# Order of the seven products in pairs of weight chunks, place of the softmax exponentials, and buffers kept between stages, in a two-layer diffusion trunk

## The chip, the core and the metric

The kernel runs on one core of one Trainium2 chip. The metric is the device time of one execution in microseconds (us), the median of several runs. Besides these there is one execution that was recorded by the hardware profiler.

## What is computed

A trunk of two layers serves 128 context tokens and 512 latent tokens, 640 columns in all, with a model width of 2048. Both layers have the same frame:

```python
h = rms_norm(x, norm_g[l]) * (1.0 + scale) + shift
y, side = even_mixer(...)  # layer 0; odd_mixer in layer 1
x = x + gate * (y @ w_out[l])
...
y = jnp.concatenate([ya, yb], axis=-1) * jax.nn.silu(gp)   # in both mixers, of h @ w_in
```

`scale`, `shift` and `gate` come from a small product of a conditioning vector (the modulation). The even mixer holds windowed attention with a sink (8 heads) and gated linear attention (4 heads). The odd mixer holds neighbourhood attention on a grid (8 heads) and a spatial gating MLP (gMLP). Each mixer's width is 2048, and its gate `gp` multiplies it. All is float32. Results are the two outputs and the keys, values and states of the context.

## The kernel before

**Chunks.** Activations lie transposed in SBUF: 16 tiles k of 128 features, 640 columns each. A weight chunk is 128 output features wide and 16 tiles k deep. Each float32 operand is split into a high and a low part, both read by TensorE in one pass: activations in `acth` and `actl` (`ah`, `al` in the code), weights in `whi` and `wlo`. A product of one tile is three matmuls of about 320 columns: `acth,whi`, `actl,whi`, `acth,wlo`. Of the weights, ScalarE (ACT) makes `whi`, then GpSimd (POOL) or VectorE (DVE) subtracts to get `wlo`; the split parts lie in a ring of 2560 columns (five pieces of 512, `RING`), so that splits run a few pieces ahead of TensorE (`wpump`, line 727). All loads are queued on SyncE, in order; a load waits there until its buffer is free, and those behind it wait too.

**Pairs.** Most chunks of the second half of the run are taken two at a time (`spair`, line 933), by a scheme of Strassen and Winograd: the tiles k are cut into a near half (0 to 7) and a far half (8 to 15), the columns into halves 1 and 2, and instead of eight half products there are seven. The two chunks c1 and c2 give four corners of weights: 11 and 12 are c1 with the near and the far half of k, 21 and 22 are c2. Sums of corners, made on VectorE by `strassen_jobs` (line 646) in five buffers of 128x1024 (`rs`, `wraw`), are S1 = 21 + 22, S2 = S1 - 11, S4 = 12 - S2, S3 = 22 - S2. The products are A11, A12, S4 and S3 with activations, and S1, S2 and A22 with three sums of activations (numbers 0, 1 and 2). `steps` (line 632) writes their order by hand. A name with a prime is the half of a product with k tiles 4 to 7 of its eight, without a prime tiles 0 to 3. Each such half is one block of 12 matmuls; a pair of full form has 14 blocks. Some pairs are of a short form (`ns` = 4), in which only 4 tiles of each half take part and the others are plain products.

The three sums of activations for tiles 0 to 3 stay in SBUF (`eh`, `el`). Those for tiles 4 to 7 lie in DRAM (`far_dram`) and come through four slots (`tail`), one set at a time: the primed halves of S1, S2 and A22 read the slots, and behind each tile the slot is loaded again with the set that the next of them needs (`far_load`, line 928). The order of a full pair is

`A11' A11 S1' S1 A12 A12' S4 S2' S2 S4' S3 S3' A22' A22`,

so each pair loads all three sets, 12 loads. There are 28 full pairs: a run of 24 in the odd layer's input projection (5 with the gMLP, 13 with the neighbourhood attention, 6 with gates) and 4 in the last output projection. `fold` (line 1101) makes the sums ahead of a run and puts one of them in the place of half 2 of the near tiles of `acth` and `actl`, for S3 (`t_dram` in the trace); the originals are kept in DRAM (`bh_dram`, `bl_dram`) and come back in `unfold` (line 1255), which is called behind the last pair of a run (lines 2425 and 2597).

Results gather in PSUM banks. Five are for the pairs (`npj`). A bank t holds A11, then S2 and S3 on top of it; between them ScalarE copies it out (`copy`, line 1008, to `sums`), after all pending evacuations were forced (`settle`). Evacuations are generators in a queue (`later`); they add the copies to the banks and pass the result to the chunk's own function (`lin`, `gate`, `out_evac`).

**Order of the work.** The whole program is laid out by a planner (`Pace`, and `tick`, line 479): TensorE's pair blocks are written in order, and behind every second tile pieces of other work (attention heads, splits, folds, the modulation) are emitted, when the planner's own estimate of engine and DMA times says that their inputs are ready. A DMA is reckoned in `dma` (line 416). `until` yields until an estimate has come; `wait` until a flag stands; `need` runs other tasks without emitting pair blocks until a flag stands.

**Heads.** Both attentions go through `blocks` (line 1674): for each block of 128 queries `s1` makes the scores and `soft1` (line 1651) the maximum `mx`, its negative `nm` on VectorE and the exponential on ScalarE; `soft2` scales; two blocks later `s3` transposes. At the end of a head, transposed blocks meet the values in matmuls of up to 512 columns (`bank<-Y 128x512` in the trace). In the neighbourhood attention, `open_na` (line 2536) first needs the gMLP to be done, closes its buffers and opens others; `open_g1` (line 2572) needs the last head, closes these, opens the gate's buffers and loads parked tiles of y.

Of the kernel before, what the change touches and what calls it, by code (L numbers as in the profile page):

```python
# [22 lines left out]
T = NCTX + NLAT  # L23
# [210 lines left out]
class Trunk:  # L234
# [177 lines left out]
    force = busy = False  # L412
# [3 lines left out]
    def dma(self, out, in_):  # L416
# [7 lines left out]
        def emit():  # L424
            at = pc.t["q"] = max(pc.t["q"], self.now, pc.ready("q", o, i)) + 0.45
            pc.t["d"] = max(pc.t["d"], at + 0.65) + max(0.09, n / 360e3)
            pc.note("q", o, i, pc.t["d"] + 1.0)
            self.nc.sync.dma_start(out, in_)  # L428
# [203 lines left out]
    def steps(c1, c2, ns):  # L632

        if ns == NS:
            todo = "A11' A11 S1' S1 A12 A12' S4 S2' S2 S4' S3 S3' A22' A22".split()
# [10 lines left out]
    def strassen_jobs(self, pairs):  # L646
# [11 lines left out]
        free[4] = len(J)  # L658
        if len(pairs) > 1:
            J.append(load(4, pairs[1][0], 0))  # L660
        for n, (c1, c2, ns, *_) in enumerate(pairs):
            one, two = (pairs[n + i] if n + i < len(pairs) else None for i in (1, 2))
            spare = ({*range(5)} - {*at.values()}).pop()
            sums = {
# [3 lines left out]
                "S3": ("21", "22", "11", ALU.subtract),  # L668
            }
            home = {"A11": "11", "A12": "12", "S1": "21", "S2": "11", "S4": "12", "S3": "21", "A22": "22"}  # L670
            when = {
                ("A11", 1): [("S1", 1), ("S2", 1)],
                ("A11", 0): [("S1", 0), ("S2", 0)],
                ("A12", 0): [("S4", 0)],
                ("A12", 1): [("S4", 1)],
                ("S4", 0): [("S3", 0)],
                ("S2", 1): [("S3", 1)],
            }
            if ns != NS:
                when = {("A12", 0): [("S1", 0), ("S2", 0)], ("S1", 0): [("S4", 0), ("S3", 0)]}  # L680
            steps = self.steps(c1, c2, ns)
            todo = list(steps)
            next_at = {"11": spare}
            for key in steps:
# [6 lines left out]
                J.append(("split", key, lambda i=at[home[f]], h=h: self.piece(i, h), 4, 128))  # L691
                for g, i in when.get((f, h), ()):
                    o, a, b, op = sums[g]
                    J.append(("add", lambda x=(at[o], at[a], at[b]), i=i: [self.piece(y, i) for y in x], op))
                if f not in [x[1] for x in todo] and f in ("S2", "S4", "S3", "A22"):
                    i = at[home[f]]
                    free[i] = len(J)
                    r = {"S2": "21", "S4": "22", "S3": "12", "A22": None}[f]
                    if r and one:
                        next_at[r] = i  # L700
                        J.append(load(i, one[int(r[0]) - 1], NS * (int(r[1]) - 1)))
                    elif r is None and two:
                        J.append(load(i, two[0], 0))
# [229 lines left out]
    def spair(self, c1, c2, ns, used, then):  # L933
# [17 lines left out]
        def tt(f):  # L951
# [31 lines left out]
        def product(b, view, key, x, again=None):  # L983
            hi, lo = self.wget(key)
            st = first(b)
            for i in range(4):
# [3 lines left out]
                if i % 2:  # L990
                    self.tick()
# [39 lines left out]
        def two(x, v):  # L1031
            yield from self.until(x)
            plus(x, half(v))
# [16 lines left out]
        t = take()  # L1050
        xa = xb = v = ya = None
        steps = self.steps(c1, c2, ns)
        for n, key in enumerate(steps):
            c, f, h = key
            last = f not in [x[1] for x in steps[n + 1 :]]
            if isinstance(f, int):
# [3 lines left out]
                else:  # L1060
                    ya = ya or take()
                    plain(key, ya, v)
                if c == c1 and f > NS:
                    later(c1, one(xa, x))
            elif f == "A11":
                product(t, full, key, J(x1))
                if last:
                    x = copy(full(t))
            elif f == "A12":
                xa = xa or take()  # L1070
                product(xa, full, key, M(x1))
                if last and ns == NS:
                    later(c1, one(xa, x))
            elif f == "S1":
# [4 lines left out]
            elif f == "S2":  # L1079
                product(t, full, key, tt(1), 2)  # L1080
                if last:
                    x = copy(half(t))
                    later(c1, two(x, v))
            elif f == "S4":
                xb = xb or take()
                product(xb, half, key, M(x2))
                if last:
                    later(c1, three_(xb, x))
            elif f == "S3":
                self.need(f"T3{h}")  # L1090
                product(t, half, key, J(x2))
                if last:
                    x = copy(full(t))
                    self.drop(t)
            else:
                ya = ya or take()
                product(ya, full, key, tt(2), 0 if then else None)
                if last:
                    later(c2, four(ya, v, x))
# [551 lines left out]
    def soft1(self, p, ps, mask, w, sinkcol):  # L1651
# [22 lines left out]
    def blocks(self, n, s1, s3, lag, hold):  # L1674
# [5 lines left out]
        for t in range(n + lag):  # L1680
# [11 lines left out]
            if t < n:  # L1692
# [4 lines left out]
                st[t] = s1(t, own[t])  # L1697
# [1198 lines left out]
```

## Time and profile before

| | |
|---|---|
| runs of the kernel before | 2179.47, 2179.72 and 2186.09 us, median 2179.72 |
| profiled execution | 2187.29 us |
| its span on the core | 2185.5 us |
| instructions | 39032 |
| HBM read and written | 403.10 MB, 38.45 MB |
| mean granted TensorE clock | 0.987 |

A profile row of a group or the timeline reads: line, engine, operation, written tile <- read tiles, shapes, count, and in brackets the idle time of that engine just before and what ended it. Line 208 is that of a helper through which all instructions of VectorE, ScalarE and GpSimd pass, 394 that of matmuls, 399 that of transposes, 428 that of loads; so tiles tell more than lines. In rows of windows stand the bounds, the width, busy time and count of TensorE's matmuls, its weight loads, VectorE, ScalarE and GpSimd, then the granted clock of TensorE (1.00 is full), the share of busy DMA time and GB/s.

### The profile page before, as it was taken

Reading aid. Unit: us, or ns where it says so; the run is one execution under the profiler, and the core shown is the slowest. Engines: PE = TensorE matmul, PEld = TensorE weight load, DVE = VectorE, ACT = ScalarE, POOL = GpSimd, SP = SyncE. Lnnn points to the kernel's source line nnn. Section 1 sums busy time; section 2 is a strip of 40 time slices with the busy share of each in tenths; the row PEclk is TensorE's granted clock in tenths of the full one; section 3 lists DMA queues with packets and bytes.
Section 4 is the critical chain, followed back from the end, with each engine's and each line's share of the span. In section 5 each row is a group of like instructions: output and inputs, shape, how many; then the busy total and the mean of one; then the engine's idle time right before and its main releaser. Section 6 shows DMA issues by size and latency. Waiting matters only on the chain.

```text
span 2185.5 us, 39032 instructions
## 1 busy us (share of the span) xinstructions
PE 2083.0 (95%) x13990; PEld 1992.6 (91%) x13990; DVE 1537.5 (70%) x3389; ACT 959.0 (44%) x2084; POOL 1021.9 (47%) x775
## 2 busy tenths in 40 slices
PE   7999999999999999999899999999999999998896
PEld 5789999999899999999899998999899899998896
DVE  1337777767887876788647877887777777665565
ACT  4425445343433445444444344444444544443343
POOL 3433233323223222566365655554545466647793
PEclk9999999999999999999999999999999999999998
DMA  9934433346445334776576677777776686665786
GB/s 375 360 135 151 130 109 99 103 129 201 135 127 175 120 117 138 242 235 204 154 241 213 226 266 245 263 242 245 242 247 215 224 286 237 217 211 193 235 273 214
DMA packets 232819, 446.76 MB, mean 204 GB/s; under 512 B 27376, under 2 KB 93744, under 8 KB 232624
## 3 DMA queue, kind: packets, MB, share of 16 engines
q1 hardware_dynamic: 231152, 442.70, 60.7%
q8 instruction: 110, 1.80, 0.3%
q10 hardware_dynamic: 1472, 1.56, 0.2%
q14 instruction: 85, 0.70, 0.1%
HBM read 403.10 MB, written 38.45 MB: 202 GB/s over the span
## 4 chain that ended last, share of the span: by engine, by line
PE 67%; DMA 11%; DVE 10%; issue 5%; POOL 3%; ACT 3%; SPq 1%; ACTq 0%; POOLq 0%; DVEq 0%
PE bank L394 64%; DMA tail<-far_dram 2%; POOL wlo L208 2%; DVE arena L208 2%; DVE Y L208 2%; PE bank L399 2%; DVE adas L208 1%; PE bank L1510 1%; DMA rs<-w_odd 1%; DVE bank L208 1%; SPq L428 1%; DMA wraw<-w_odd 1%; DMA adas<-ada_g 1%; DVE wlo L208 1%; DVE actl L208 1%
## 5 line engine op out<-in xcount | busy, mean ns | idle before, releaser
L394 PE MATMUL bank<-acth,whi 128*128 128x320 f32 (+1 forms) x3144 | 968.4, 319 | 24.5 <-DMA acth<-bh_dram 6.5
L394 PE MATMUL bank<-acth,wlo 128*128 128x320 f32 (+1 forms) x3144 | 942.4, 311 | 4.9 <-POOL wlo L208 3.2
L394 PE MATMUL bank<-actl,whi 128*128 128x320 f32 (+1 forms) x3144 | 941.0, 311 | 1.5 <-DMA actl<-bl_dram 1.5
L208 POOL TENSOR_TENSOR wlo<-wraw,whi 128x512 fp32r<-128x512 f32 x370 | 518.2, 1409 | 781.2 <-ACT whi L208 668.9
L394 PEld LDWEIGHTS bank<-acth,whi 128*128 128x128 f32 x3144 | 586.1, 189 | 44.1 <-ACT whi L208 7.3
L394 PEld LDWEIGHTS bank<-acth,wlo 128*128 128x128 f32 x3144 | 585.0, 189 | 7.9 <-POOL wlo L208 5.1
L394 PEld LDWEIGHTS bank<-actl,whi 128*128 128x128 f32 x3144 | 586.2, 189 | 3.4 <-DMA actl<-bl_dram 1.9
L208 POOL TENSOR_TENSOR wlo<-rs,whi 128x512 fp32r<-128x512 f32 x244 | 343.0, 1417 | 257.6 <-ACT whi L208 209.7
L208 ACT ACTIVATE whi<-wraw 128x512 fp32r<-128x512 f32 (+1 forms) x429 | 261.7, 623 | 166.6 <-PE bank L394 94.7
L208 ACT ACTIVATE whi<-rs 128x512 fp32r<-128x512 f32 x297 | 179.2, 623 | 76.3 <-PE bank L394 41.1
L208 DVE CUSTOM_DVE_ANT_0 adas<-adas,bank,partg 128x256 bf16<-128x256 f32 (+1 forms) x320 | 178.1, 557 | 19.9 <-ACT bank L208 7.1
L394 PE MATMUL bank<-tail,whi 128*128 128x322 f32 (+1 forms) x672 | 159.2, 323 | 16.4 <-DMA tail<-far_dram 11.1
L394 PE MATMUL bank<-eh,wlo 128*128 128x322 f32 (+1 forms) x444 | 139.4, 314 | 1.8 <-DVE wlo L208 1.2
L394 PE MATMUL bank<-eh,whi 128*128 128x322 f32 (+1 forms) x444 | 141.0, 318 | 0.0
L394 PE MATMUL bank<-el,whi 128*128 128x322 f32 (+1 forms) x444 | 138.8, 313 | 0.0
L394 PEld LDWEIGHTS bank<-tail,whi 128*128 128x128 f32 x672 | 112.8, 192 | 25.0 <-DMA tail<-far_dram 16.5
L208 ACT ACTIVATE Y<-bank 128x128 f32<-128x128 f32 (+5 forms) x134 | 52.4, 411 | 135.7 <-PE bank L394 82.8
L208 ACT ACTIVATE bc<-bank 128x2 f32<-128x2 f32 (+1 forms) x101 | 17.1, 170 | 210.8 <-DVE arena L208 124.3
L394 PE MATMUL bank<-tail,wlo 128*128 128x322 f32 (+1 forms) x336 | 105.7, 315 | 3.5 <-POOL wlo L208 3.5
L208 DVE TENSOR_TENSOR rs<-rs 128x512 f32<-128x512 f32 x81 | 90.3, 1125 | 25.6 <-POOL wlo L208 19.5
L208 DVE TENSOR_TENSOR wlo<-wraw,whi 128x512 fp32r<-128x512 f32 x59 | 62.8, 1066 | 62.7 <-ACT whi L208 57.5
L208 DVE TENSOR_TENSOR bank<-bank,sums 128x320 f32<-128x320 f32 (+1 forms) x148 | 69.6, 493 | 40.0 <-PE bank L394 39.6
(215 smaller groups left out, 2952.1 us busy)
## 6 DMA issues: line engine op xcount, KB each, us to landing
tail<-far_dram SPq DMA_DIRECT2D x288, 322.0 KB, 4.8
wraw<-w_even SPq DMA_DIRECT2D x176, 256.0 KB, 3.2
adas<-ada_g SPq DMA_DIRECT2D x128, 256.0 KB, 4.4
adas<-ada SPq DMA_DIRECT2D x128, 256.0 KB, 3.7
rs<-w_odd SPq DMA_DIRECT2D x60, 512.0 KB, 6.5
wraw<-w_odd SPq DMA_DIRECT2D x40, 512.0 KB, 6.0
Y<-ada SPq DMA_DIRECT2D x37, 512.0 KB, 6.7
rs<-w_out SPq DMA_DIRECT2D x30, 512.0 KB, 4.7
```

The costliest lines, as they stand in the source:

```text
L208: return f(*args, **kw)
L394: self.nc.tensor.matmul(out, lhsT, rhs, start=start, stop=stop, **kw)
L399: self.nc.tensor.transpose(out, in_, self.ident[:k, :k])
L428: self.nc.sync.dma_start(out, in_)
L1510: nc.tensor.matmul(o, c, w[:, j, :], start=(q == 0), stop=(q == 3))
```

## The change

**Alternating pairs.** The full pairs of a run now have three orders: an opening pair (`back` None), then pairs that run backward and forward in turn (`back` True and False):

```diff
-            todo = "A11' A11 S1' S1 A12 A12' S4 S2' S2 S4' S3 S3' A22' A22".split()
+            if back is None:
+                todo = "A11' A11 A12 A12' S1' S1 S4' S4 S2 S2' S3 S3' A22 A22'".split()
+            else:
+                todo = "A11' A11 A12 A12' S2' S2 S4' S4 S3 S3'".split()
+                todo = ["A22'", *todo, "A22", "S1", "S1'"] if back else ["S1'", "S1", *todo, "A22", "A22'"]
```

A forward pair ends with set 2 of the far sums in the slots, and the backward pair that follows begins with it; a backward pair ends with set 0, with which the forward one begins. Each of them loads two sets, 8 loads.

```diff
-                product(t, full, key, tt(1), 2)
+                product(t, full, key, tt(1), 0 if back else 2)
...
-                product(ya, full, key, tt(2), 0 if then else None)
+                product(ya, full, key, tt(2), 1 if back else None)
```

In a backward pair S1 comes last and is added to bank t, so that t is copied four times, not three, and the results of c1 and c2 are put together by other generators (`five`, `six`, `seven`):

```diff
+            elif f == "S1" and back:
+                product(t, half, key, tt(0, 2))
+                if last:
+                    x = copy(half(t))
+                    later(c1, six(xb, x))
+                    later(c2, seven(t))
```

The loads of corners go in the order in which the next pair needs them, and S1 of a forward pair is added on VectorE while the pair before it is still under way, behind the split of A22:

```diff
+        order = lambda p: ("11", "21", "22", "12") if p[4] is None else ("22", "11", "21", "12") if p[4] else ("21", "22", "11", "12")
...
+                if back and (f, h) == ("A22", 1):
+                    add("S1", 1)
+                    add("S1", 0)
...
+                if one and one[4] is False and key == steps[-3]:
+                    add("S1", 1, next_at)
+                    add("S1", 0, next_at)
```

On SyncE, in the gate stage of the odd layer, the loads of the far sums (`tail`) and of corners (`rs`, `wraw`) stood before as:

```order
L428 DMA tail_10968<-far_dram 128x644 x12
L428 DMA wraw<-w_odd 128x1024
L428 DMA rs_7767<-w_odd 128x1024 x2
L428 DMA wraw<-w_odd 128x1024
L428 DMA tail_10968<-far_dram 128x644 x8
L428 DMA rs_7767<-w_odd 128x1024
L428 DMA tail_10968<-far_dram 128x644 x2
```

Now, in the same stage:

```order
L428 DMA tail_11102<-far_dram 128x644 x8
L428 DMA rs_7781<-w_odd 128x1024 x3
L428 DMA wraw<-w_odd 128x1024
L428 DMA tail_11102<-far_dram 128x644 x8
L428 DMA rs_7781<-w_odd 128x1024 x2
L428 DMA wraw<-w_odd 128x1024
L428 DMA tail_11102<-far_dram 128x644 x8
```

Between as many corner loads there are fewer far loads; over the program 336 became 232.

**Unfolding.** It is started behind S3 of a run's last pair and no longer behind that pair:

```diff
+                    if end:
+                        self.spawn(self.unfold(), first=True)
...
-            do(lambda: (self.turn_tail(False), self.spawn(self.unfold(), first=True)))
+            do(lambda: self.turn_tail(False))
```

At the end of layer 0's output projection, SyncE's rows were (the returned originals are `bh_dram` and `bl_dram`, `x1T_dram` is the spill of x):

```order
L428 DMA wraw<-w_out 128x512
L428 DMA tail_81<-x1T_dram 128x640
L428 DMA x1T_dram<-arena_7774 128x640
L428 DMA tail_81<-x1T_dram 128x640
L428 DMA arena_7774<-xT 128x640
L428 DMA acth<-bh_dram 128x320
L428 DMA actl<-bl_dram 128x320
```

and are now, from the last of the returned tiles on:

```order
L428 DMA acth<-bh_dram 128x320
L428 DMA actl<-bl_dram 128x320
L428 DMA adas<-crow_s 128x2x256
L428 DMA wraw<-w_out 128x512
L428 DMA tail_81<-x1T_dram 128x640
L428 DMA x1T_dram<-arena_7788 128x640
L428 DMA tail_81<-x1T_dram 128x640
L428 DMA arena_7788<-xT 128x640 x2
```

The returned tiles moved ahead of the last spill and of the two loads around it.

**Exponentials.** `soft1` is a generator now and yields until the planner's time for nm has come, before it emits the exponential:

```diff
+        yield from self.until(nm)
         self.act(p[:, :w], p[:, :w], AF.Exp, bias=nm, accum_out=den)
```

**Planner.** A DMA's reckoned time grows:

```diff
-            pc.t["d"] = max(pc.t["d"], at + 0.65) + max(0.09, n / 360e3)
+            pc.t["d"] = max(pc.t["d"], at + 1.2) + max(0.09, n / 330e3)
```

**Buffers in place.** The neighbourhood heads use the gate's buffers (`ssq`, `last`, `xr`) and no others are opened; the flags "gmlp" and "nh7" are waited for by the tasks and evacuations that touch the buffers, and the parked tiles of y are loaded by a task:

```diff
         def open_na():
-            self.need("gmlp")
-            self.close_arena()
-            self.arena(4.61)
-            L["hq"], L["hk"] = self.take(T, 2), self.take(T, 2)
+            L["hq"], L["hk"] = Ring([self.ssq, self.last[:, :T]]), Ring(self.xr.list)
...
         def open_g1():
-            self.need("nh7")
-            self.close_arena()
-            for i in range(4):
-                self.dma(Y[:, 8 + i, :], ysp[:, i, :])
-            for i in range(6):
-                self.dma(Y[:, 2 + i, :], self.hsp[:, i, :])
-            self.open_gate()
+            def homes():
+                yield from self.wait("nh7")
+                for i in range(4):
+                    self.dma(Y[:, 8 + i, :], ysp[:, i, :])
+                    self.flags.add(f"home{8 + i}")
+                    yield
...
+            self.spawn(homes(), first=True)
```

Where the last head ends, TensorE's rows were (`eh` is a block of S2 or A22 or S1; `ident` are transposes of the head's last block, then come its products with the values):

```order
L394 MATMUL bank_70<-eh_7765,wlo 128x322
L399 MATMUL bank_73<-ident,arena_12619 128x128
L399 MATMUL bank_73<-ident,arena_12619 64x128
L399 MATMUL bank_73<-ident,arena_12619 128x128
L394 MATMUL bank_72<-Y 128x512
L394 MATMUL bank_72<-Y 128x128
L394 MATMUL bank_72<-Y 128x256 x3
L394 MATMUL bank_72<-Y 128x128
L394 MATMUL bank_69<-acth,whi 128x322
```

and are now:

```order
L394 MATMUL bank_68<-eh_7779,wlo 128x322
L399 MATMUL bank_72<-ident,Y 128x128 x3
L399 MATMUL bank_73<-ident,arena_7788 128x128
L399 MATMUL bank_73<-ident,arena_7788 64x128
L399 MATMUL bank_73<-ident,arena_7788 128x128
L394 MATMUL bank_72<-Y 128x512
L394 MATMUL bank_72<-Y 128x128
L394 MATMUL bank_72<-Y 128x256 x3
L394 MATMUL bank_72<-Y 128x128
L394 MATMUL bank_69<-acth,whi 128x320
```

They moved from the border between the last pair with attention and the first with gates to the middle of the latter, and the transposes of the block before the last have come next to them.

More of the change, by code (lines that the diff above doesn't have):

```diff
@@ L411 @@
     share, soon = 0.0, 99.0
-    force = busy = False
+    force = busy = often = False
     lags2, cap2 = (8.0, 6.0, 4.0, 1.0, 0.4), 2.0
@@ L658, in strassen_jobs @@
         free[4] = len(J)
+        order = lambda p: ("11", "21", "22", "12") if p[4] is None else ("22", "11", "21", "12") if p[4] else ("21", "22", "11", "12")
+        corner = lambda i, p, r: load(i, p[int(r[0]) - 1], NS * (int(r[1]) - 1))
         if len(pairs) > 1:
-            J.append(load(4, pairs[1][0], 0))
-        for n, (c1, c2, ns, *_) in enumerate(pairs):
+            J.append(corner(4, pairs[1], order(pairs[1])[0]))
+        for n, pair in enumerate(pairs):
+            c1, c2, ns, _, back = pair
             one, two = (pairs[n + i] if n + i < len(pairs) else None for i in (1, 2))
             spare = ({*range(5)} - {*at.values()}).pop()
+            last = "11" if back else "21"
             sums = {
@@ L680, in strassen_jobs, with add @@
                 when = {("A12", 0): [("S1", 0), ("S2", 0)], ("S1", 0): [("S4", 0), ("S3", 0)]}
-            steps = self.steps(c1, c2, ns)
+            elif back is None:
+                when["A11", 1].insert(0, ("S1", 1))
+                when["A11", 0].insert(0, ("S1", 0))
+            steps = self.steps(c1, c2, ns, back)
             todo = list(steps)
-            next_at = {"11": spare}
+            rest = list(order(one)) if one else []
+            next_at = {rest.pop(0): spare} if one else {}
+            def add(g, i, at=at):
+                o, a, b, op = sums[g]
+                J.append(("add", lambda x=(at[o], at[a], at[b]): [self.piece(y, i) for y in x], op))
             for key in steps:
@@ L1029, in one, with two @@
             self.drop(xa)
-        def two(x, v):
-            yield from self.until(x)
-            plus(x, half(v))
+        def two(x, y):
+            yield from self.until(x, y)
+            plus(x, y)
         def three_(xb, x):
@@ L1048, in four, with five, six, seven @@
             self.drop(ya, v)
-        t = take()
-        xa = xb = v = ya = None
-        steps = self.steps(c1, c2, ns)
+        def five(ya, xb, x):
+            yield from self.until(x)
+            plus(full(ya), x)
+            nc.vector.tensor_tensor(half(xb), half(xb), half(x), ALU.subtract)
+            yield from ev(c2, ya, None)
+            self.drop(ya)
+        def six(xb, x):
+            yield from self.until(x)
+            plus(half(xb), x)
+            yield from ev(c1, None, half(xb))
+            self.drop(xb)
+        def seven(t):
+            yield from ev(c2, None, half(t))
+            self.drop(t)
+        t = xa = xb = v = ya = None
+        steps = self.steps(c1, c2, ns, back)
         for n, key in enumerate(steps):
@@ L1079, in spair @@
             elif f == "S2":
-                product(t, full, key, tt(1), 2)
+                product(t, full, key, tt(1), 0 if back else 2)
                 if last:
                     x = copy(half(t))
-                    later(c1, two(x, v))
+                    if not back:
+                        later(c1, two(x, half(v)))
+                    if back is None and ns == NS:
+                        later(c1, three_(xb, x))
             elif f == "S4":
@@ L1086, in spair @@
                 product(xb, half, key, M(x2))
-                if last:
-                    later(c1, three_(xb, x))
+                if last and (back is not None or ns != NS):
+                    later(c1, two(half(xb), x) if back else three_(xb, x))
             elif f == "S3":
@@ L2550, in open_na @@
             L["nk"] = Ring([yt(1, 256) for _ in range(2)])
-            self.pieces = [yt(1, 384) for _ in range(3)] + [self.take(384)]
+            self.pieces = [yt(1, 384) for _ in range(3)] + [self.last[:, T:]]
         do(open_na)
```

83 lines of the change are left out of this document (46 added, 37 removed).

## The prediction

> **What bounds the kernel now.** I read the page first, then the list of who waited for whom on TensorE, then the timeline around the longest waits, then windows for the price of a wait. From the page:
>
> ```profile
> span 2185.5 us, 39032 instructions
> PE 2083.0 (95%) x13990; PEld 1992.6 (91%) x13990; DVE 1537.5 (70%) x3389; ACT 959.0 (44%) x2084; POOL 1021.9 (47%) x775
> ```
>
> TensorE (PE) works 2083 of 2185.5 us. The order of both kernels holds the same number of matmuls, so only the 102 idle us and the time at a reduced clock can change. The list of waits names who ended the idle time (us in total, times, longest):
>
> ```profile
> PE bank L394 <- DMA tail<-far_dram: 11.1, 9, 4.2
> PE bank L394 <- ACT whi L208: 9.9, 7, 3.2
> PE bank L394 <- POOL wlo L208: 7.2, 9, 1.4
> PE bank L394 <- DMA acth<-bh_dram: 6.5, 2, 4.3
> ```
>
> No one wait rules: the top row is the reload of the far operands, rows two and three are weights split too late, the last the unfolding. The timeline puts the longest waits in their places (start, duration, idle before in brackets):
>
> ```profile
> 1058.69 0.63 PE L394 MATMUL bank<-acth,whi 128*128 128x320 f32 x1 [4.31 <-DMA acth<-bh_dram]
> 1061.09 0.64 PE L394 MATMUL bank<-actl,whi 128*128 128x320 f32 x1 [1.50 <-DMA actl<-bl_dram]
> 1911.80 0.58 PE L394 MATMUL bank<-acth,whi 128*128 128x320 f32 x1 [2.19 <-DMA acth<-bh_dram]
> 2035.54 0.56 PE L394 MATMUL bank<-tail,whi 128*128 128x320 f32 x2 [1.05 <-DMA tail<-far_dram]
> 2040.49 0.90 PE L394 MATMUL bank<-tail,whi 128*128 128x320 f32 x2 [4.24 <-DMA tail<-far_dram]
> ```
>
> A wait costs more than its idle time. In the windows the first number behind the bounds is the width, the second TensorE's busy time with its matmuls, the last but two the granted clock:
>
> ```profile
> 1030.00:1050.00 20.00, 20.00 (x138) 20.00 (x137) 13.03 (x50) 8.49 (x16) 13.57 (x11) 1.00 0.47 148
> 1059.00:1066.00 7.00, 5.50 (x22) 5.10 (x22) 0.82 (x1) 0.74 (x1) 0.00 (x0) 0.54 0.78 176
> 1242.00:1248.00 6.00, 6.00 (x37) 6.00 (x36) 3.35 (x4) 1.48 (x3) 3.49 (x3) 0.72 0.07 11
> 1354.00:1360.00 6.00, 5.02 (x22) 4.75 (x23) 1.81 (x5) 0.63 (x1) 1.27 (x1) 0.72 1.03 377
> 1553.00:1559.00 6.00, 5.21 (x28) 4.89 (x28) 3.18 (x8) 1.83 (x5) 3.91 (x3) 0.72 0.52 150
> 1912.00:1918.00 6.00, 6.00 (x31) 5.99 (x32) 1.02 (x2) 1.70 (x3) 0.00 (x0) 0.72 0.92 298
> 1976.00:1982.00 6.00, 5.59 (x28) 5.33 (x27) 5.86 (x5) 3.15 (x6) 5.92 (x6) 0.72 0.32 112
> 2040.00:2046.00 6.00, 5.51 (x24) 5.51 (x24) 0.00 (x0) 1.26 (x2) 1.94 (x2) 0.58 0.74 258
> ```
>
> The first window is undisturbed: 20 us / 138 = 0.145 us a matmul, so a block of 12 is 1.74 us. In the others, busy time x (1 - clock) is lost on top of the wait: 5.50 x 0.46 = 2.5 us, then 1.7, 1.4, 1.5, 1.7, 1.6 and 2.3 us.
>
> The Trainium skill, TensorE: Matmul & The Clock Gate, section "What's actually happening", says that the clock falls to half after at least one idle window of about 3.4 us. This trace differs: 0.72 stands after an idle of only 2.19 us. By that rule only the waits of 4.31 and 4.24 us would cost clock, the clock's part of the sum below (8.9 us) would be 3.5, and the result 2161 us.
>
> **The change part by part.** The sum is made against the profiled execution (2187.3 us, span 2185.5); the median of the runs, 2179.7, lies 7.6 lower, and I take what is saved off that.
>
> *Unfolding earlier.* SyncE's timeline shows why it was late:
>
> ```profile
> 1050.98 0.33 SPq L428 DMA_DIRECT2D x1T_dram<-arena  x1
> 1054.39 0.32 SPq L428 DMA_DIRECT2D tail<-x1T_dram  x1
> 1055.28 0.39 SPq L428 DMA_DIRECT2D acth<-bh_dram  x1
> ```
>
> The load stood behind a load that waited for a spill, and was issued 0.9 us after TensorE had run dry (1058.69 - 4.31 = 1054.38). Now it is queued after S3 of the last pair and ahead of those two. What is left of that pair is a plain block of 24 matmuls and A22, 36 x 0.145 = 5.2 us; at the second place, whose pair runs backward, A22, S1 and S1', 5.2 us too. The waits were 4.31 + 1.50 and 2.19, with 2.5 + 1.7 of clock: 12.2 us. I take 11, since 5.2 doesn't quite cover 5.8. Bounds 6 (VectorE is late next at the first place) and 12.
>
> *Alternating pairs.* TensorE keeps its 168 matmuls a pair. The far loads fall from 336 to 232. The rows for landing (KB each, us):
>
> ```profile
> tail<-far_dram SPq DMA_DIRECT2D x288, 322.0 KB, 4.8
> rs<-w_odd SPq DMA_DIRECT2D x60, 512.0 KB, 6.5
> ```
>
> Before, A22' reloaded its slots three blocks ahead of S1', 5.2 us against 4.8 for landing: no margin. Now the shortest distance is four blocks (A22' to S2' backward), 7.0 us, the others five to seven; three remain only once, in each opening pair. So I take away all tail waits but those of the run that opens the last projection: 11.1 - (1.05 + 4.24) = 5.8, and 1.4 of clock. In that opening pair S1' now comes 24 matmuls later, behind A12: 3.5 of its 5.3 us go, and 1 of 2.3 of clock. Together 11.7; bounds 7 (the opening pair gains nothing) and 15 (its wait goes whole).
>
> Its costs. In the opening pair S3 follows S2' on the same bank with nothing between, so TensorE waits for ScalarE's copy: 0.42 us of copy (the sums row below) and the way there and back, 0.7 x 2 pairs = 1.4 us. Backward pairs copy once more, 14 x 0.42 = 5.9 us on ScalarE, hidden in its 56% idle time; uncovered it would be the whole 5.9. A forward pair's S1 is now added in the pair before, after the split of A22, and its corner 22 is loaded only after the split of S4, three splits earlier: 3 x 1.74 = 5.2 us against 6.5 for landing. Before, five splits lay between. The nearest rows are VectorE's waits for such corners:
>
> ```profile
> DVE rs L208 <- DMA rs<-w_odd: 5.0, 3, 2.9
> DVE wraw L208 <- DMA wraw<-w_odd: 4.5, 3, 1.8
> DVE rs L208 <- DMA wraw<-w_odd: 3.9, 2, 3.5
> DVE wraw L208 <- DMA rs<-w_odd: 2.7, 2, 2.5
> ```
>
> That is 16.1 / 10 = 1.6 us each; at 12 borders 19 us of VectorE. Queued behind the waiting add are evacuations, for which ScalarE and the next splits wait. Five weight slots ahead of TensorE (2560 / 512, some four blocks, 7 us) cover most; I let a quarter through, 5 us, with bounds 0 and 52 (the first rival).
>
> *Exponentials when their maximum is ready.* ScalarE waited for that maximum (nm) often, and once TensorE can be seen behind it:
>
> ```profile
> ACT arena L208 <- DVE nm L208: 89.4, 47, 4.5
> ACT Y L208 <- DVE nm L208: 53.7, 30, 4.3
> 1550.59 0.56 ACT L208 ACTIVATE arena<-arena,nm 128x320 f32<-128x320 f32 x1 [1.35 <-DVE nm L208]
> 1552.72 0.57 PE L394 MATMUL bank<-tail,whi 128*128 128x322 f32 x2 [2.13 <-ACT whi L208]
> ```
>
> The split of the weights (whi) stood behind the exponential on ScalarE: 2.13 us and 1.5 of clock, 3.6. Of 143 us of such waiting the rest is hidden; I add 1.4 for both attention stages and take 5. Bounds 2 and 12. The added wait is the generator's, not an engine's: a head gets longer by the ticks until nm is there. What then is late is the end of a head.
>
> *Longer DMA times in the planner.* ScalarE's conversions were queued before the store that still read their tile had landed:
>
> ```profile
> 1971.78 0.47 ACT L208 ACTIVATE Y<-adas 128x320 fp32r<-128x320 f32 x1 [3.57 <-DMA far_dram<-Y]
> 1975.70 0.41 PE L394 MATMUL bank<-acth,whi 128*128 128x320 f32 x1 [3.17 <-ACT whi L208]
> 2017.54 0.47 ACT L208 ACTIVATE Y<-Y 128x320 fp32r<-128x320 f32 x1 [6.11 <-DMA t_dram<-Y]
> 2018.28 0.42 ACT L208 ACTIVATE sums<-bank 128x320 f32<-128x320 f32 x1
> 2019.27 0.41 PE L394 MATMUL bank<-acth,whi 128*128 128x320 f32 x1 [2.63 <-DVE sums L208]
> ```
>
> 3.17 + 1.6 + 2.63 = 7.4 us hang on this. The planner's allowance grows by 0.55 us and a little per byte, less than these ScalarE waits: I take half, 4; bounds 0 and 7.4.
>
> *Buffers in place.* The first removed pause leaves no long wait of its own in the timeline. At the second stands
>
> ```profile
> 1744.42 1.90 PE L394 MATMUL bank<-Y 128*128 128x512 f32 x2 [3.74 <-ACT Y L208]
> ```
>
> but the order after shows the last head's final transposes and products still without pair products between, now forced by a gate that is evacuated; I count nothing. The same happens newly at the end of head 2: between nothing and 3.74 us, I take 1.5.
>
> Sum: 11 + 11.7 + 5 + 4 - 1.4 - 5 - 1.5 = 23.8 us. 2187.3 - 23.8 = 2163.5 for the profiled execution, 2179.7 - 23.8 = 2156 for the median.
>
> **The rivals.**
> *Corner 22 comes too late (slower).* If landing with the wait for GpSimd ahead of it takes longer than 5.2 us plus the cover of 7, VectorE stands, evacuations and splits behind it, and TensorE waits at every forward border. The price is that of the worst weight wait in the trace:
>
> ```profile
> 1239.78 0.42 PE L394 MATMUL bank<-acth,whi 128*128 128x322 f32 x1 [1.16 <-ACT whi L208]
> 1241.79 0.42 PE L394 MATMUL bank<-acth,wlo 128*128 128x322 f32 x1 [1.44 <-POOL wlo L208]
> ```
>
> 1.16 + 1.44 + 1.7 of clock = 4.3 us, x 12 = 52, against savings of 31.7 - 2.9 = 28.8: 2179.7 + 23.2 = 2203. It decides from 2.4 us a border. Against it: 6.5 us for landing lies far below 12.
>
> *Gains given back at the transitions.* With the data there, the first place waits for VectorE (7 of its 8.3 us come back), and the exponentials and planner's times bring nothing, as new orders bring their own collisions: 23.8 - 7 - 9 = 7.8 saved, 2172.
>
> *The weight waits go as well.* Four sums in a row after A11 become two, spread over the pair. Then of 9.9 + 7.2 those not counted yet (less 2.13 and 3.17) go, 11.8, with 1.7 of clock, and the 5 at the borders: 18.5 more, 2137.
>
> **How the numbers follow.** Mine 0.44, gains given back 0.22, weight waits too 0.24, corner late 0.10. A measurement of this kernel can tell some 0.3% (6.5 us) from no change; given back lies at 7.8, so over a third of it falls within: faster 0.81, same 0.10, slower 0.09. The range runs from 2134, a little under the weight rival, to 2176, a little above the given-back one.
>
> **What would show it.** Right: the two waits for bh_dram gone or under 1 us; the tail row at 2 to 3 us and only in the last projection; the nm rows of ScalarE near nothing; clock losses at fewer places. Wrong: VectorE's rows for corner loads far above 35 us with whi waits at each forward border; or new whi, sums or transposition waits of a us or two spread over the attention stage, which eat what the loads gave.

## The result and the profile after

The changed kernel takes 2151.57 us (median of four runs, 2148.37 to 2152.63), the kernel before 2181.45 us beside it: a ratio of 0.9858, with a 95% interval of 0.9837 to 0.9878. That is 30 us saved where 23.8 were forecast, inside the range. The profiled execution took 2151.12 us against 2187.29 before, 36.2 less; some 6 us of that are scatter, since the profiled execution before lay 5.8 us above the median of its kernel and the one after 0.5 us below.

The first lines of the page after:

```profile
span 2149.3 us, 38899 instructions
PE 2069.3 (96%) x13990; PEld 1985.7 (92%) x13990; DVE 1533.2 (71%) x3383; ACT 964.8 (45%) x2100; POOL 1033.0 (48%) x781
```

The matmuls are the same in number. TensorE's idle time fell from 102.5 to 80.0 us, its busy time by 13.7 us. The list of waits on TensorE after (us in total, times, longest):

```profile
PE bank L394 <- POOL wlo L208: 10.1, 17, 1.2
PE bank L394 <- ACT whi L208: 8.1, 7, 3.9
...
PE bank L394 <- DMA tail<-far_dram: 6.5, 2, 5.1
...
PE bank L394 <- DVE tail L208: 3.9, 1, 3.9
```

The rows for `bh_dram` and `bl_dram` are gone; the far operands' row fell from nine waits to two. New are more and shorter waits for `wlo`, and one for VectorE's `tail`. The timeline has the long ones in their places:

```profile
1082.16 0.78 PE L394 MATMUL bank<-acth,whi 128*128 128x322 f32 x2 [3.92 <-DVE tail L208]
1941.14 0.63 PE L394 MATMUL bank<-acth,whi 128*128 128x320 f32 x1 [3.93 <-ACT whi L208]
2005.32 0.90 PE L394 MATMUL bank<-tail,whi 128*128 128x320 f32 x2 [5.14 <-DMA tail<-far_dram]
```

To see where the time went, I cut both executions at three marks that stand in every trace with the same matmuls between them: the matmul behind a wait of 1.3 us for `arena` early in each output projection (1 and 3), and the matmul behind the first wait for `whi` of the odd layer's input projection (2). In each row behind the bounds stand the width, then TensorE's busy time with its matmuls, as in the prediction. Between the marks, before:

```profile
859.10:1106.90 247.80, 238.98 (x1582) 235.23 (x1582) 188.13 (x443) 114.00 (x245) 126.27 (x105) 0.99 0.64 203
1106.90:1938.00 831.10, 797.50 (x5203) 767.81 (x5203) 624.21 (x1387) 376.93 (x844) 452.41 (x326) 0.99 0.71 240
1938.00:2185.50 247.50, 217.27 (x1423) 213.20 (x1423) 144.32 (x204) 97.90 (x192) 170.51 (x138) 0.95 0.70 233
```

After:

```profile
857.40:1103.00 245.60, 237.64 (x1581) 234.56 (x1581) 187.48 (x432) 112.79 (x243) 124.53 (x101) 0.99 0.64 199
1103.00:1902.70 799.70, 781.55 (x5203) 759.71 (x5203) 626.93 (x1369) 381.95 (x858) 475.70 (x340) 1.00 0.64 212
1902.70:2149.30 246.60, 217.25 (x1423) 213.27 (x1423) 146.22 (x209) 97.59 (x194) 161.11 (x133) 0.96 0.66 217
```

The second row of each is the finding: of 36 us, 31.4 come from the stretch 2 to 3, which holds the 24 pairs of the odd layer with the neighbourhood attention beside them. There idle time fell by 15.4 us (831.10 - 797.50 = 33.6, then 18.2). In windows of 1 us, busy time x (1 - clock) adds up to 11.2 us of lost clock there before and 1.7 after. Of the waits in that stretch, those for ScalarE's `Y` fell from 7.3 to 1.9 us, for `whi` from 6.7 to 2.5, for the far operands from 5.4 to 1.4, and the 2.2 us for `bh_dram` went; those for VectorE's `arena` rose from 0.6 to 3.6. The stretch with the first unfolding gave 2.2 us, the last projection 0.9.

### The profile page after: what moved, and what is told of

Its sections match the earlier page's. It is cut to its first block, busy times and chain, and to the rows that moved or that the text cites. A ratio compares the mean times of both kernels' runs of the same rounds, so it can differ in the third digit from the quotient of the medians.

```text
span 2149.3 us, 38899 instructions
## 1 busy us (share of the span) xinstructions
PE 2069.3 (96%) x13990; PEld 1985.7 (92%) x13990; DVE 1533.2 (71%) x3383; ACT 964.8 (45%) x2100; POOL 1033.0 (48%) x781
## 5 line engine op out<-in xcount | busy, mean ns | idle before, releaser
L208 POOL TENSOR_TENSOR wlo<-wraw,whi 128x512 fp32r<-128x512 f32 x345 | 480.3, 1399 | 749.5 <-ACT whi L208 648.3
L394 PEld LDWEIGHTS bank<-acth,whi 128*128 128x128 f32 x3144 | 584.5, 189 | 41.2 <-ACT whi L208 10.8
L208 POOL TENSOR_TENSOR wlo<-rs,whi 128x512 fp32r<-128x512 f32 x275 | 393.4, 1444 | 238.3 <-ACT whi L208 196.4
L208 ACT ACTIVATE whi<-wraw 128x512 fp32r<-128x512 f32 (+1 forms) x397 | 242.6, 623 | 161.3 <-PE bank L394 84.5
L208 ACT ACTIVATE whi<-rs 128x512 fp32r<-128x512 f32 x329 | 197.6, 623 | 57.9 <-PE bank L394 35.3
L394 PE MATMUL bank<-tail,whi 128*128 128x322 f32 (+1 forms) x672 | 152.5, 314 | 6.6 <-DMA tail<-far_dram 6.5
L208 DVE TENSOR_TENSOR bank<-bank,sums 128x320 f32<-128x320 f32 (+1 forms) x162 | 76.5, 493 | 36.7 <-PE bank L394 28.9
L208 ACT ACTIVATE arena<-arena,bc 128x192 f32<-128x192 f32 (+4 forms) x167 | 82.3, 517 | 42.6 <-DVE arena L208 40.9
L208 DVE TENSOR_TENSOR rs<-rs 128x512 f32<-128x512 f32 x83 | 84.4, 1025 | 21.2 <-POOL wlo L208 20.5
```

The source lines that it names most:

```text
L208: return f(*args, **kw)
L394: self.nc.tensor.matmul(out, lhsT, rhs, start=start, stop=stop, **kw)
```

## The experiments

I took the change apart into alternating pairs (A), early unfolding (B), exponentials that wait for their maximum (C), longer DMA times in the planner (D) and buffers in place (E). The runs were made in three groups, each with the kernel before beside it (2184.48, 2185.74 and 2183.01 us); ratios are to it. My theory was the forecast's: each part brings its term (A 5.3 net, B 11, C 5, D 4, E nothing, less 1.5). The rivals were that the gains are given back in other places, and that the parts depend on each other.

**One part taken out of the changed kernel: B, C, D.** B: `unfold` is spawned behind the last pair again.

```diff
-                    if end:
-                        self.spawn(self.unfold(), first=True)
...
+            do(lambda: (self.turn_tail(False), self.spawn(self.unfold(), first=True)))
```

> The changed kernel with unfolding started behind the last pair of a run, as before. By the forecast it costs 11 us, 2163, with waits for bh_dram of some 6 and 2 us and their clock. By the rival that this gain is given back at the transition (a wait of 3.9 us for VectorE's tail tile stands there now, with 1.7 of clock), it costs 5 to 6, 2157, and that wait shrinks.

2167.82 us, ratio 0.993 (0.9909 to 0.9951): 16 us slower than the changed kernel. Three places of its TensorE timeline:

```profile
1057.93 0.63 PE L394 MATMUL bank<-acth,whi 128*128 128x320 f32 x1 [5.07 <-DMA acth<-bh_dram]
1139.13 0.90 PE L394 MATMUL bank<-acth,whi 128*128 128x322 f32 x2 [4.62 <-ACT whi L208]
1890.81 0.41 PE L394 MATMUL bank<-acth,whi 128*128 128x320 f32 x1 [2.92 <-DMA acth<-bh_dram]
```

Both loads are waited for again. The row between them is a collision that no other kernel here shows above 1.4 us at this place, among them three that unfold late too (before, and the two with alternating below): so I put it down to this order of the queued work and not to the load, and a part of the 16 us with it.

C: the exponential is emitted at once again, and the callers no longer hand the waiting on.

```diff
-        yield from self.until(nm)
         self.act(p[:, :w], p[:, :w], AF.Exp, bias=nm, accum_out=den)
```

> The changed kernel with the exponential emitted at once, as before. By the forecast 5 us slower, 2157, with ScalarE's nm rows near 143 us and single whi waits of TensorE behind them. By the rival that nearly all of this waiting was hidden: within 2 us of 2151.6.

2157.52 us, ratio 0.9878 (0.9861 to 0.9894): 5 to 6 us slower. The intervals of the ratios overlap, but its four runs (2155.45 to 2157.64) all lie above all nine of the changed kernel (2144.79 to 2154.22). In its list the weight waits are larger than in that of the changed kernel:

```profile
PE bank L394 <- POOL wlo L208: 14.5, 21, 1.2
PE bank L394 <- ACT whi L208: 11.1, 8, 5.4
```

D: the planner reckons loads as before.

```diff
-            pc.t["d"] = max(pc.t["d"], at + 1.2) + max(0.09, n / 330e3)
+            pc.t["d"] = max(pc.t["d"], at + 0.65) + max(0.09, n / 360e3)
```

> The changed kernel with the planner's old DMA times. By the forecast 4 us slower, 2156, with ScalarE waiting longer for t_dram and far_dram stores and a sums or whi wait of 2 to 3 us back in the last projection. By the rival that half a microsecond is too little to matter, within 2 us of 2151.6.

2147.44 us, ratio 0.9838 (0.9816 to 0.9859): not slower. But its stretches differ, and this is the more telling result:

```profile
1099.20:1895.60 796.40, 782.51 (x5203) 759.68 (x5203) 613.47 (x1387) 384.27 (x861) 473.01 (x344) 1.00 0.64 214
1895.60:2151.50 255.90, 221.51 (x1423) 216.76 (x1423) 152.36 (x210) 97.11 (x194) 163.44 (x132) 0.93 0.64 210
```

The last projection is 9.3 us longer than in the changed kernel (255.9 against 246.6); in it a wait of the kernel before is back:

```profile
1977.20 0.41 PE L394 MATMUL bank<-acth,whi 128*128 128x320 f32 x1 [3.71 <-DVE sums L208]
```

The attention stretch, in another order, was 3.3 us shorter than in the first profile of the changed kernel, and the rest lies within what the runs scatter.

**Alternating taken out.** All full pairs run in the order of before; `back`, `five`, `six` and `seven` go.

```diff
-            if back is None:
...
+            todo = "A11' A11 S1' S1 A12 A12' S4 S2' S2 S4' S3 S3' A22' A22".split()
```

> The changed kernel with the old order of products and of corner loads; unfolding, exponentials, planner and buffers as changed. By the forecast's terms (11.7 for far loads, less 1.4 and 5 of costs) the time rises by 5.3 us over the changed kernel's 2151.6, to 2157, with tail waits of 5 us or more back and far loads at 336. By the rival that the weight waits went through the spread of the sums (whi and wlo short waits, with clock), it rises by some 20, to 2171, and whi and wlo waits in the attention stage come back.

2147.45 us, ratio 0.983 (0.981 to 0.985), as quick as the changed kernel. This run is not to be read as it stands: with part A, I had taken out one line more, `self.settle()` ahead of the plain products of short pairs, so one addition in each short pair reads its bank at another moment than it should. So I ran it again with that line, beside a control, and once more, in the next group, without part D:

```diff
                 else:
                     ya = ya or take()
+                    self.settle()
                     plain(key, ya, v)
```

> The changed kernel once more, as the control on the chip that runs the three kernels sent with it. Both theories expect a ratio to the kernel before of 0.984 to 0.988 (2149 to 2155 us). If it comes out at 0.983 or below, the gains seen without the alternating order and without the longer DMA times (0.983 and 0.984) were differences between chips and not of the kernels.

> The changed kernel with all pairs in the old order, as in the first such run, but with the one line kept that lets queued work go ahead of a plain product, so that the whole computation is done. Theory of the parts (alternating brings nothing by itself, since the early unfolding and the standing buffers already take the load queue's congestion away): within 3 us of the control, ratio 0.983 to 0.987. Theory of the forecast (alternating is worth 5 us net: 11.7 less 1.4 less 5): 5 us over the control, ratio 0.988 or more. Rival that the missing line made the first run quick: more than 5 us over the control too, but with the tail row no larger than in the control.

> The changed kernel with the pairs in the old order (the settling line kept) and also with the planner's shorter DMA times, which were worth nothing when taken out alone: a second order of the queued work without alternating. Theory that alternating is worth 12 us beside the other parts: ratio 0.989 to 0.992, tail row of 10 us or more. Theory of the chance order (the 12 us were a bad draw of the planner, the 17 us between the two runs without alternating show how far draws lie apart): 0.983 to 0.987.

| kernel | us, median | ratio, 95% interval |
|---|---|---|
| the changed kernel again | 2152.44 | 0.9845 (0.9821 to 0.9869) |
| without alternating | 2164.78 | 0.9910 (0.9888 to 0.9932) |
| without alternating and longer DMA times | 2161.63 | 0.9906 (0.9892 to 0.9921) |

Without alternating the kernel is 12 us slower than the control, and in the second order 14 us slower than the kernel that lacks only the longer DMA times (2147.44, from another group). So alternating is not worth nothing beside the other parts, as I had begun to think. The rival of a chance order didn't come in this second order. But two orders are few, and the first run, one line away, lies 17 us from the first of them: how much of the 12 to 14 us alternating itself brings is not settled. What alternating was made for are the far loads; without it (the first of the two) their row reads:

```profile
PE bank L394 <- DMA tail<-far_dram: 13.7, 6, 5.9
```

13.7 against 6.5 us in the changed kernel: 7 of the 12 us are these waits. In the second order it stands at 17.7 us, against 7.0 in the kernel without the longer DMA times.

**One part or two in the kernel before.** The same hunks of the diff, put into the kernel before: alternating alone, alternating with the exponentials' wait, and early unfolding alone.

> The kernel before with nothing changed but the alternating order of the pairs (unfolding at its old place). Forecast: 5 us quicker than before, ratio 0.9976, the tail row at 3 us. Theory of the parts (the order is worth nothing, the tail waits go but others come in their place): 0.998 to 1.002. Rival that the order helps as long as the other parts don't cover for it: tail waits and their clock go as in the forecast's 11.7 and no corner cost appears, ratio 0.994 or less.

2185.81 us against 2185.74: ratio 1.0002 (0.9986 to 1.0018). Nothing. Its waits and its last two stretches:

```profile
PE bank L394 <- POOL wlo L208: 14.1, 24, 1.2
PE bank L394 <- ACT whi L208: 10.1, 10, 4.0
PE bank L394 <- DMA tail<-far_dram: 9.3, 3, 5.2
```

```profile
1107.60:1931.60 824.00, 792.68 (x5204) 763.16 (x5204) 626.42 (x1389) 378.80 (x855) 467.76 (x338) 0.99 0.62 206
1931.60:2184.40 252.80, 219.87 (x1423) 214.86 (x1423) 150.52 (x210) 97.15 (x194) 163.04 (x132) 0.95 0.64 212
```

Inside the run of 24 pairs the far loads stop TensorE once and not six times, at S2' of a forward pair:

```profile
1753.64 0.54 PE L394 MATMUL bank<-tail,whi 128*128 128x322 f32 x2 [2.95 <-DMA tail<-far_dram]
```

The whole row, 9.3 us, is far from the 3 of the forecast. The stretch is 7.1 us shorter, 2.3 of it idle time and 4.8 busy time (the lost clock there falls from 11.2 to 6.3 us). But `wlo` is waited for 24 times, not 9, and the last projection is 5.3 us longer: what one stretch gave, the other took.

> The kernel before with two parts of the change: alternating pairs and the exponentials that wait for their maximum. Theory of the shared split (alternating alone gave nothing, since short waits for the weights' low part came in the place of the far loads' waits, as ScalarE's split stood behind exponentials that waited for their maximum): the wlo row falls from 14.1 to 9 us or less, and the two together give more than the exponentials' 5 us, 10 to 14 us, ratio 0.9936 to 0.9955. Theory of plain addition (0 + 5): ratio 0.997 to 0.998, wlo row at 12 us or more.

2168.65 us, ratio 0.9937 (0.9923 to 0.9951), 14 us quicker than before. On TensorE and on ScalarE:

```profile
PE bank L394 <- POOL wlo L208: 6.6, 11, 1.2
```

```profile
ACT arena L208 <- DVE nm L208: 35.1, 23, 3.7
```

```profile
1107.20:1916.50 809.30, 787.17 (x5204) 763.94 (x5204) 611.04 (x1381) 379.73 (x855) 478.58 (x346) 0.99 0.63 210
```

As expected of the theory of the shared split: with the exponentials off ScalarE's queue until `nm` is there, the `wlo` row falls from 14.1 to 6.6 us, and the attention stretch from 824.0 to 809.3. The last projection stays at 253.5. The far loads' row is 10.8 us, hardly smaller than in the kernel before. The exponentials' wait alone in the kernel before was not run, so how much of these 14 us it would bring without alternating stays open. It may be most of them: the kernel with unfolding alone (below) and the changed one without alternating and longer DMA times differ only in the exponentials' wait and the buffers, alternate in neither, and lie 11 us apart in the same group (2173.08 and 2161.63).

> The kernel before with nothing changed but the early unfolding (and the settling line, without which short pairs would run their work in another order). Forecast: 11 us, ratio 0.995, both rows for bh_dram and bl_dram gone. Theory from the run without it (16 us, since the wait of 4 to 5 us also upsets what is queued behind): ratio 0.9915 to 0.9935. Rival (part of those 16 us needs the other parts): 0.996 or more, with a wait for VectorE or whi of 3 to 5 us at 1070 to 1110 in the place of the load's.

2173.08 us, ratio 0.995 (0.9931 to 0.9969): 10 to 11 us, as forecast, with both loads' rows gone.

**Buffers as before.** Part E taken out, of which these lines are the core:

```diff
+            self.need("gmlp")
+            self.close_arena()
+            self.arena(4.61)
+            L["hq"], L["hk"] = self.take(T, 2), self.take(T, 2)
-            L["hq"], L["hk"] = Ring([self.ssq, self.last[:, :T]]), Ring(self.xr.list)
```

> The changed kernel with the buffers of the neighbourhood attention and of the gates taken and given back as before. Theory of the forecast (worth nothing): within 2 us of the control, ratio 0.986. Theory of the parts (what is left of the 30 us after 16 for the unfolding and 5 for the exponentials lies here): 8 to 10 us over the control, ratio 0.990, with new waits of 1 to 4 us for whi, Y or arena where the neighbourhood attention begins (about 1330) and ends (about 1730), and with clock losses there.

2155.92 us, ratio 0.9869 (0.9847 to 0.9891), 3.5 us over the control by the medians; the intervals overlap, so that it isn't resolved. The stretch 2 to 3 takes 807.9 us, against 799.7 and 803.3 in the two profiles of the changed kernel, and the far loads' row 11.2 us in six waits, against 5.9 in two in the control. The 8 to 10 us of the theory of the parts didn't come.

**The opening pair.** One edit to the changed kernel, with `need("Tf")` moved to the half that reads the slots:

```diff
-                todo = "A11' A11 A12 A12' S1' S1 S4' S4 S2 S2' S3 S3' A22 A22'".split()
+                todo = "A11' A11 A12 A12' S1 S1' S4' S4 S2 S2' S3 S3' A22 A22'".split()
```

> The changed kernel with one edit: in each opening pair S1 runs ahead of S1', so that the product that needs the reloaded far operands comes 12 matmuls (1.74 us) later. Theory of the late load (the 5.15 us at 2000 are the far loads' landing, a fixed time after A11 has run): that wait falls to 3.4 us, 2 to 3 us in all with its clock, ratio 0.983. Rival (the loads are issued or run later by as much, as the DMA engines are the limit there): the wait stays at 4.8 us or more and the time at that of the changed kernel.

The wait fell by 2.3 us, from 5.14 to 2.88, as expected of a late load:

```profile
2006.89 0.90 PE L394 MATMUL bank<-tail,whi 128*128 128x320 f32 x2 [2.88 <-DMA tail<-far_dram]
```

2149.05 us, ratio 0.9846 (0.983 to 0.9861): in its time not told apart from the changed kernel, since 2 us are less than the runs scatter. Apart from the first run without alternating, the quickest kernel here is the one without longer DMA times, 2147.44 us, and its four runs (2144.93 to 2153.33) lie among those of the changed kernel.

**All of them by stretch.** Each figure is the difference of the starts of two marks in the timeline of one profiled execution; the two profiles of the changed kernel show by how much one kernel varies.

| kernel | 1 to 2 | 2 to 3 | 3 to end |
|---|---|---|---|
| before | 247.8 | 831.2 | 247.5 |
| alternating alone | 248.5 | 824.0 | 252.8 |
| unfolding alone | 244.0 | 814.9 | 255.5 |
| alternating + exponentials | 249.6 | 809.3 | 253.5 |
| after without alternating and D | 241.6 | 811.8 | 250.7 |
| after without alternating | 243.2 | 812.9 | 249.7 |
| after without alternating, one line less (the first run) | 242.2 | 804.5 | 244.9 |
| after without early unfolding | 247.3 | 812.9 | 247.8 |
| after without the exponentials' wait | 240.2 | 810.1 | 246.9 |
| after without buffers in place | 243.8 | 807.9 | 245.9 |
| after without longer DMA times | 243.9 | 796.4 | 255.9 |
| after with S1 ahead of S1' in the opening pair | 245.4 | 803.7 | 242.8 |
| after, two profiles | 245.6, 242.6 | 799.7, 803.3 | 246.6, 247.0 |

## Why the prediction was right, point by point

**The sum and its places.** 23.8 us were forecast and 30 measured, so the median came out 4.4 us under the forecast. The total hides errors of both signs. By its own terms the forecast had put some 8 us at the first transition (4.31 + 1.50 + 2.5), 8.5 in the last projection (3.5 + 1 + 4) and 9 net in the odd layer's run (3.9 + 7.2 + 5, less 5, 1.5 and 0.7); the profiles show 2.2, 0.9 and 31.4. That the total came near is in good part luck.

**Unfolding.** Its total came out as sized when alone (10 to 11 of 11), and as 16 beside the other parts. Both loads are waited for no longer. At the first place the lower bound came true: TensorE now waits 3.92 us for VectorE and loses 1.7 of clock behind it, so of 8.3 us only some 2 to 5 are won (247.8 against 245.6 and 242.6). That alone would make the term some 6 us; the rest came in the run of pairs (831.2 to 814.9 with the unfolding alone), where only 3.9 us of waits and clock could be named beforehand, and the last projection gave 8.0 back (247.5 to 255.5). So 3.8, 16.3 and -8.0 us add up to the 11 of the forecast by chance. I read this as another order of the queued work with fewer collisions; which of them the unfolding itself removed isn't shown.

**Alternating pairs.** Inside the run, 5.8 us of waits and 1.4 of clock were to go, 7.2 (0.4 of the 5.8 stood in the last projection); alternating alone shortened that stretch by 7.1. This agreement is luck too: the far loads' waits there fell by only 2.4 us, from 5.4 to 3.0, and the lost clock by 4.9. The tail row was to end at 2 to 3 us in the last projection alone; it stands at 6.5, with one wait in the odd layer:

```profile
1204.87 0.56 PE L394 MATMUL bank<-tail,whi 128*128 128x322 f32 x2 [1.36 <-DMA tail<-far_dram]
```

That is A22' of the run's opening pair, where three blocks lie behind S2'; the prediction names this place and counts nothing for it. The copy between S2' and S3 cost 0.53 us in each of the two opening pairs (at 1196.51 and 2016.69), 1.1 for the 1.4 taken. The step that failed is the opening pair, in which "3.5 of its 5.3 us go": 5.14 us stayed. SyncE's timeline after shows why:

```profile
1990.86 0.32 SPq L428 DMA_DIRECT2D far_dram<-tail  x1
1992.79 0.88 SPq L428 DMA_DIRECT2D tail<-far_dram  x2
...
1994.94 0.42 SPq L428 DMA_DIRECT2D tail<-far_dram  x1
1995.40 0.47 SPq L428 DMA_DIRECT2D acth<-t_dram  x1
...
1999.32 0.32 SPq L428 DMA_DIRECT2D arena<-x1T_dram  x1
1999.70 2.77 SPq L428 DMA_DIRECT2D tail<-far_dram  x4
```

The loads of three slots go out by 1994.94. The fourth slot's load goes out at 1999.70, behind eight other loads that take SyncE 0.3 to 0.5 us each, and TensorE goes on 5.6 us later, at 2005.32. The blocks put ahead of S1' bought little. Counted from the pair's first matmul (at 2029.12 before, 1991.57 now), the fourth load went out after 6.4 us before and after 8.1 now, and landed in 4.9 and 5.6 us, so that 2.4 of the 3.5 us were lost again. From the last spill to TensorE's stop it is 9.3 us (1990.86 to 2000.18), and it was 8.4 in the trace of before (2027.89 to 2036.25). I had moved the reader and taken the writer to stay. A fourth load ahead of the other eight was not tried.

**Corner 22.** No price of it shows on TensorE, where 5 us were allowed for, and the rival built on it didn't come. VectorE's waits for corners of the odd layer fell from 16.1 to 9.7 us; the last projection has a new one (the last row), behind which TensorE waited no more than 0.24 us:

```profile
DVE rs L208 <- DMA wraw<-w_odd: 3.2, 3, 1.6
DVE wraw L208 <- DMA rs<-w_odd: 3.0, 3, 1.9
...
DVE rs L208 <- DMA rs<-w_odd: 2.3, 4, 1.1
...
DVE wraw L208 <- DMA wraw<-w_odd: 1.2, 2, 0.7
...
DVE wraw L208 <- DMA wraw<-w_out: 3.8, 1, 3.8
```

In neither profile of the changed kernel does TensorE wait for `whi` or `wlo` in S1' or S1 of a forward pair. Three short waits return in the gate stage, 50 us apart, but they stand at S4' of the backward pairs 20, 22 and 24, behind S2:

```profile
1759.98 0.41 PE L394 MATMUL bank<-acth,wlo 128*128 128x320 f32 x1 [0.28 <-POOL wlo L208]
1810.20 0.41 PE L394 MATMUL bank<-acth,wlo 128*128 128x320 f32 x1 [0.28 <-POOL wlo L208]
1860.47 0.41 PE L394 MATMUL bank<-acth,wlo 128*128 128x320 f32 x1 [0.28 <-POOL wlo L208]
```

Before the first of them ScalarE's split (1757.93) stood behind a small copy, `bc`, that had waited 4.04 us for VectorE's `arena`.

**Exponentials.** Sized right: 5 forecast, 5 to 6 measured. ScalarE's waits for `nm` fell from 143 to 38 us, not to near nothing:

```profile
ACT arena L208 <- DVE nm L208: 32.1, 24, 3.1
...
ACT Y L208 <- DVE nm L208: 5.9, 5, 2.6
```

The mechanism was seen too narrowly. I looked for one long wait (2.13 us and its clock); what the run without it shows are many short ones, 14.5 us for `wlo` in 21 waits, against 10.1 in 17. Over all kernels here the `wlo` row stands at 14.1 and 14.5 us where the pairs alternate and the exponentials don't wait, at 6.6 to 10.1 where both are done, and at 5.1 to 7.2 without alternating, whether the exponentials wait or not. So these waits come with alternating, and the exponentials' wait takes a good part of them away again. In the stretch 2 to 3, TensorE's busy time less its lost clock is 784 to 787 us in the four kernels without the wait, and 779 to 783 in all others; of the 16.0 us by which busy time fell there, 9.5 are clock, and the other 6.5, most of which come with the exponentials, stand in no row.

**Longer DMA times.** 4 us were forecast, and the whole kernel without them is not slower. In the stretch where the forecast put them, they show: the last projection takes 243 to 250 us in the seven kernels of the table with them (eight profiles), 251 to 256 in five of the six without them, and 247.5 in the kernel before. Only one of the two waits went, the 2.63 us for `sums`: the same matmul waits 1.3 to 3.7 us for it in all six kernels without the longer times and in none of the seven with them. The other, 3.17 us for `whi`, is 3.93 now, and 0.55 us more in the planner's reckoning are little against a store for which ScalarE still waits 7.5 us at the longest:

```profile
ACT Y L208 <- DMA far_dram<-Y: 12.9, 3, 7.5
```

**Buffers in place, and head 2.** Nothing was counted for the buffers; 3.5 us were measured, not resolved. The forced end of head 2 costs 0.94 us, near the 1.5 taken. At the end of the last head the 3.74 us for `Y` are gone, and a transposition there waits 2.90 us for `arena` (at 1729.60).

**The clock rule.** With the rule cited in the prediction the sum would have given 2161, farther from 2151.57 than the trace's own prices. That says little, as the sum had its places wrong; the windows at the end speak against it directly.

**The weight waits** did not go as well: `whi` and `wlo` together took 17.1 us before and 18.2 after.

## What to carry to other kernels

In a kernel whose bound engine is 95% busy, waits that are named and priced can give a total of the right size and still have its places wrong: cut the trace at common marks before trusting the terms. For each wait that is to go, ask what is late next, and look at the queue of the load itself, not only at its reader. Parts need not add up (alternating gave 0 alone, 12 to 14 us in company), so take a part out of the whole as well as putting it in alone. And where a planner lays out the work, any edit gives a new order: trust a few us only if more than one order shows them.

## What the runs showed that was not expected

The spread between orders. The first kernel without alternating and the one with the settling line differ in one line, hold the same matmuls in nearly the same order, and lie 17 us apart (2147.45 and 2164.78, ratios 0.983 and 0.991).

Whether a short wait costs clock differs from one execution to the next. The same two waits, 1.33 + 0.80 us and 1.28 + 0.80 us, and the windows behind them, in the second profile of the changed kernel:

```profile
1329.00 0.41 PE L394 MATMUL bank<-acth,whi 128*128 128x320 f32 x1 [1.33 <-ACT whi L208]
1330.36 0.41 PE L394 MATMUL bank<-acth,wlo 128*128 128x320 f32 x1 [0.80 <-POOL wlo L208]
```

```profile
1331.00:1335.00 4.00, 4.00 (x19) 4.00 (x18) 2.29 (x5) 1.27 (x3) 3.93 (x3) 0.57 0.66 180
```

And in the first:

```profile
1332.98 0.41 PE L394 MATMUL bank<-acth,whi 128*128 128x320 f32 x1 [1.28 <-ACT whi L208]
1334.34 0.41 PE L394 MATMUL bank<-acth,wlo 128*128 128x320 f32 x1 [0.80 <-POOL wlo L208]
```

```profile
1335.00:1339.00 4.00, 4.00 (x29) 4.00 (x28) 3.38 (x9) 1.88 (x4) 4.00 (x4) 1.00 0.62 194
```

The same length of time held 19 matmuls at a granted clock of 0.57 and 29 at 1.00. The Trainium skill, TensorE: Matmul & The Clock Gate, section "What's actually happening", names an idle window of about 3.4 us as the condition; the execution with 0.57 disagrees with it, at 1.33 + 0.80 us.
